# Projections of a hybrid S5 and attention layer: TensorE in program order, late transpositions, gate blocks in between, and a recurrence that steps through PSUM

## The chip, the cores and the metric

The kernel runs on one core of one Trainium2 chip. The metric is the device time of one execution in microseconds (us). Before the change it is 2119.36 us (median of 3 runs, 2116.5 to 2119.44).

## The reference

One layer over 1024 latent tokens and 256 context tokens of width 1024, in fp32. Both are normalised and modulated (shift and scale come from a small "ada" projection of a condition), and one input projection yields everything else:

```
z = modulate(x, ...) @ w_in            # q 1024 | k 1024 | v 1024 | u 512 | gates g 2048
q = rope_2d(rms_norm(q)); k = rope_2d(rms_norm(k))      # 8 heads x 2 maps x 64
y_attn = diff_attention(q, [kc, k], [vc, v])            # two softmax maps per head, subtracted
s_t = a_bar * s_(t-1) + B u_t          # S5: complex diagonal state, 32 groups x 64, both directions
y_s5 = glu(gelu(Re(C s) + D u)) @ w_branch_s5
x = x + ga1 * ((sigmoid(g_s) * y_s5 + sigmoid(g_a) * y_attn) @ w_out)
x = x + ga2 * conv_ffn(modulate(x, ...))                # up, depthwise conv of 3, silu gate, down
```

The context tokens give keys, values and the S5 start state only; they have no q and no gates.

## The kernel before

Every fp32 product is made of three fp32r matmuls: each operand is split in a high and a low part (hi*hi, hi*lo, lo*hi). A weight block of 512 KB is read into `wraw`, ScalarE (ACT) rounds it to `whi` (L596), GpSimd (POOL) subtracts to get `wlo` (L597, 128x1024). The normalised input lies transposed in SBUF as `hTh`/`hTl` (latent) and `cTh`/`cTl` (context).

The part that changes is the first 40% of the program, `phase_a`. It works through column slabs of 512:

- U (10 token tiles of 128), then K in two slabs (20 tiles), V in two slabs (20), Q in two slabs of latent tokens only (16). One tile is one `project` call: 24 matmuls 128x512 into a PSUM bank `z` (L418 to L420).
- A K or Q tile then goes through `qk_post` (L635 to L681). ACT squares it (L640), VectorE (DVE) sums per head (L642), makes 1/sqrt with a Newton step (L643 to L650, ACT's Sqrt at L646 in between), multiplies by the rope tables (L654, L658), POOL adds (L659), ACT and POOL scale (L664, L665), TensorE (PE) transposes four pieces (L669), ACT and DVE split the result (L672, L673), and it goes to memory.
- Beside U and K run the S5 parameters, one quad of groups at a time (`s5_params`): complex products on DVE or POOL (L753 to L758), transposes L846, small matmuls L864. Beside V run the S5 inputs per chunk of 8 tokens (`s5_states_in`, L893, L898, L919).
- The recurrence over 160 chunks is `s5_scan`: 158 steps one after the other, each four DVE operations of 128x64 (L936 to L939), two products with the constants `A8a` and `A8b` and two sums. All operands lie in SBUF. Its calls stand between the V and the Q tiles. `ada_part` (L297, groups of 4 matmuls) stands between the Q tiles.
- The gates: 32 blocks of 24 matmuls (L555 to L557), each followed by a Tanh on ACT (L559). Between them stand the S5 outputs (`s5_out_quad`, L957 to L966, which need the finished scan), and then `s5_tail`: a GELU, the GLU (4x2 GEMMs of 12 matmuls, L1267 to L1269) and the S5 branch projection in "units" of 12 matmuls, each multiplied with a gate read back from memory (L1312).

After it come attention and the feed-forward part, which the change does not touch. The order on each engine is made by a scheduler that simulates the program; `high_priority` lets a piece go first. Attention and feed-forward have PE in the order in which they are written. PSUM has 8 banks: in `phase_a` two for transposes (`ta`, `tb`), five `z`, one `ada`.

Of the kernel before, what the change touches and what calls it, by code (L numbers as in the profile page):

```python
# [10 lines left out]
F32R = mybir.dt.float32r  # L11
# [45 lines left out]
def pack(x, c, ctx, c_ctx, ada_w, ada_b, norm1_w, w_in, b_gate, q_norm_w, k_norm_w,  # L57
# [18 lines left out]
    def perm64(a):  # L76
# [6 lines left out]
             wq[:, :512], wq[:, 512:]] + [w[:, 3584 + 512 * j:4096 + 512 * j] for j in range(4)]  # L83
# [28 lines left out]

    put("wglu", wtiles(np.asarray(glu_w)[0]))
# [25 lines left out]
class Kern:  # L139
# [81 lines left out]
    def consts(self):  # L221
        nc, cp = self.nc, self.cp
        self.small = self.t(cp, [P, NSM], "small")
        self.ident = self.t(cp, [P, P], "ident")
        self.ones = self.t(cp, [P, P], "ones")
# [8 lines left out]
        self.scan_at = 0  # L234
# [52 lines left out]
    def ada_part(self, pool, ps, crep, grp):  # L287
# [3 lines left out]
        for k in range(KT):  # L291
            for h in range(2):
                a = self.t(pool, [P, 2, 512], "araw", 2)
                nc.sync.dma_start(a, self.I["ada"][grp - 1, k][:, 2 * h:2 * h + 2])
                for z in range(2):
                    r0 = 32 * (2 * h + z)
                    nc.tensor.matmul(pa[r0:r0 + 32], crep[:, k], a[:, z], start=k == 0, stop=k == KT - 1,  # L297
                                     tile_position=(0, r0))
                yield
# [13 lines left out]
    def phase_a(self):  # L313
        nc, cp, I = self.nc, self.cp, self.I
        self.psT, self.psT_st = self.pool("psT", space=PSUM)
        ps, ps_st = self.pool("psA", space=PSUM)
        ca, ca_st = self.pool("ca")
# [3 lines left out]
        self.A8a = self.t(ca, [P, 2, G], "A8a")  # L321
        self.A8b = self.t(ca, [P, 2, G], "A8b")
# [88 lines left out]
        def project(tt, W, pz=None, ks=range(KT)):  # L411
            pz = self.t(ps, [P, 512], "z", 5) if pz is None else pz
# [85 lines left out]
        for tt in range(NKT):  # L498
            u = stage(first[tt] if tt < TA else project(tt, W))
            if tt < NT:  # L500
                nc.scalar.dma_start(self.Ud[:, tt], u)
            else:
                nc.scalar.dma_start(self.Ucd[(tt - NT) * P:(tt - NT + 1) * P], u)
            if tt % 2:
                next(params, None)
        zp, zp_st = self.pool("pk")
        self.rope_tables(zp, "K")
        for s in (0, 1):
            W = self.load_slab(wp, s)
# [4 lines left out]
        zp_st.close()  # L514
        for _ in params:
            pass
        xp, xp_st = self.pool("s5x")
        states = self.s5_states_in(xp, ps)
        next(states)
        for s in (2, 3):  # L520
            W = self.load_slab(wp, s)
            for tt in range(NKT):
                v = stage(project(tt, W))
                nc.scalar.dma_start(self.Vd[tt][:, (s - 2) * 512:(s - 1) * 512], v)
                if s > 2 or tt > 3:
                    next(states, None)
                if self.scan_at:
                    self.s5_scan(xp, self.scan_at + 10)
        hc_st.close()
        ap_, ap_st = self.pool("pada", "right")  # L530
        zp, zp_st = self.pool("pq")
        self.rope_tables(zp, "Q")
        adas = (st for grp in (1, 2) for st in self.ada_part(ap_, ps, crep, grp))
        for s in (5, 6):
            W = self.load_slab(wp, s)
            for tt in range(NT):
                self.qk_post(zp, ps, project(tt, W), "Q", s - 5, tt)
                next(adas, None)
                self.s5_scan(xp, self.scan_at + 6)
# [5 lines left out]
        for s in range(7, 11):  # L545
            W = self.load_slab(wp, s)
            for mm in range(4):
                m = (s - 7) * 4 + mm
                for hf in range(2):
                    tok = slice(hf * 512, hf * 512 + 512)  # L550
                    pz = self.t(ps, [P, 512], "z", 5)
                    for k in range(KT):
                        wh = W[0][k // 2][:, k % 2, mm * P:mm * P + P]
                        wl = W[1][k // 2][:, k % 2, mm * P:mm * P + P]
                        nc.tensor.matmul(pz, wh, hTh[k][:, tok], start=k == 0, stop=False)  # L555
                        nc.tensor.matmul(pz, wh, hTl[k][:, tok], start=False, stop=False)
                        nc.tensor.matmul(pz, wl, hTh[k][:, tok], start=False, stop=k == KT - 1)  # L557
                    g = self.t(gp, [P, 512], "stage", 2)
                    nc.scalar.activation(g, pz, AF.Tanh, scale=0.5, bias=self.hbg[:, m:m + 1])  # L559
                    nc.scalar.dma_start(self.Gd[m][:, tok], g)  # L560
                    next(adas, None)
                    if hf and nq < QUADS:
                        if nq % 2 == 0:
                            Yq = self.t(yp, [P, NT, P], "Yq", 1)
                        with self.tc.high_priority():
                            self.s5_out_quad(yp, ps, nq, Yq, xp)
                            nq += 1
# [17 lines left out]
        for _ in tail:  # L585
            pass
# [1122 lines left out]
```

## Time and profile before

| | before |
|---|---|
| median of 3 runs | 2119.36 us |
| profiled execution, device time | 2117.7 us |
| its span, first to last instruction | 2115.9 us |
| PE busy | 2016.6 us (95%) |
| DVE busy | 1364.6 us (64%) |
| POOL busy | 915.0 us (43%) |
| ACT busy | 840.7 us (40%) |
| mean granted TensorE clock | 0.978 |

The span is shorter than the device time by 1.8 us. "Busy" adds up the time in which an engine has an instruction in work. A PE that is busy can still be slow: a matmul at half the clock counts as busy for twice as long. So the stages are read in three numbers: length, PE busy, granted clock.

In the trace the stages lie so: U to about 107 us, K to 283, V to 418, Q to 537, gates to 807 with the S5 outputs at 613 to 673, GLU and units 694 to 821, and then attention.

### The profile page before, as it was taken

Reading aid. Unit: us, or ns where it says so; the run is one execution under the profiler, and the core shown is the slowest. Engines: PE = TensorE matmul, PEld = TensorE weight load, DVE = VectorE, ACT = ScalarE, POOL = GpSimd, SP = SyncE. Lnnn points to the kernel's source line nnn. Section 1 sums busy time; section 2 is a strip of 40 time slices with the busy share of each in tenths; the row PEclk is TensorE's granted clock in tenths of the full one; section 3 lists DMA queues with packets and bytes.
Section 4 is the critical chain, followed back from the end, with each engine's and each line's share of the span. In section 5 each row is a group of like instructions: output and inputs, shape, how many; then the busy total and the mean of one; then the engine's idle time right before and its main releaser. Section 6 shows DMA issues by size and latency. Waiting matters only on the chain.

```text
span 2115.9 us, 29038 instructions
## 1 busy us (share of the span) xinstructions
PE 2016.6 (95%) x10392; PEld 1643.8 (78%) x10392; DVE 1364.6 (64%) x2591; ACT 840.7 (40%) x1509; POOL 915.0 (43%) x1009
## 2 busy tenths in 40 slices
PE   6988999998999999999999989987999999999999
PEld 4766778866678887999999878765888888878887
DVE  6988944799972133888888654468777777752222
ACT  4434424221222312788888611343444443432100
POOL 1466411233311531366666745643544444455321
PEclk9998999999999999999999999987999999999999
DMA  9345575345667326322331135432222222254212
GB/s 325 111 112 140 123 204 182 111 133 163 186 198 232 112 100 225 112 83 78 94 107 53 39 131 177 151 90 70 100 80 79 82 82 79 80 193 129 67 55 93
DMA packets 164624, 262.48 MB, mean 124 GB/s; under 512 B 28672, under 2 KB 92544, under 8 KB 164480
## 3 DMA queue, kind: packets, MB, share of 16 engines
q1 hardware_dynamic: 154400, 242.28, 37.0%
q10 hardware_dynamic: 10080, 18.35, 2.3%
q8 instruction: 82, 1.34, 0.3%
q14 instruction: 62, 0.51, 0.1%
HBM read 188.68 MB, written 71.89 MB: 123 GB/s over the span
## 4 chain that ended last, share of the span: by engine, by line
PE 70%; DVE 21%; DMA 4%; issue 3%; POOL 1%; ACT 1%; SPq 0%; DVEq 0%; ACTq 0%; POOLq 0%
PE ta L1040 7%; PE d L1268 4%; PE d L1269 4%; PE d L1267 4%; PE up L1488 4%; PE up L1489 4%; PE up L1487 4%; PE sc L1240 3%; PE sc L1241 3%; PE z L1487 3%; PE z L1489 3%; PE z L1488 3%; PE tb L1022 3%; DVE X L939 2%; DVE sc L936 2%
## 5 line engine op out<-in xcount | busy, mean ns | idle before, releaser
L1242 DVE TENSOR_REDUCE mx<-sc 128x1 f32<-128x1280 f32 x128 | 190.7, 1491 | 53.3 <-PE sc L1241 52.3
L597 POOL TENSOR_TENSOR wlo<-wraw,whi 128x1024 fp32r<-128x1024 f32 x40 | 97.3, 2449 | 245.8 <-ACT whi L596 243.8
L418 PE MATMUL z<-whi,hTh 128*128 128x512 f32 x448 | 183.1, 413 | 3.6 <-ACT hTh L407 3.6
L419 PE MATMUL z<-wlo,hTh 128*128 128x512 f32 x448 | 181.7, 407 | 0.3 <-POOL wlo L597 0.3
L420 PE MATMUL z<-whi,hTl 128*128 128x512 f32 x448 | 179.9, 403 | 0.0
L995 ACT ACTIVATE e<-sc,mx 128x1280 f32<-128x1280 f32 x128 | 171.9, 1343 | 12.3 <-DVE mx L1242 10.6
L1664 DVE SCALAR_TENSOR_TENSOR x1b<-d,modT,x1b 128x512 f32<-128x512 f32 x80 | 59.8, 750 | 181.3 <-PE d L1269 181.3
L1040 PE MATMUL ta<-V,at 128*128 128x128 f32 x1280 | 168.1, 275 | 0.7 <-ACT at L1029 0.7
L1040 PEld LDWEIGHTS ta<-V,at 128*128 128x128 f32 x1280 | 155.4, 191 | 1.0 <-ACT at L1029 0.9
L1240 PE MATMUL sc<-K,q 128*128 128x512 f32 (+1 forms) x384 | 147.7, 385 | 0.8 <-ACT e L995 0.8
L1480 POOL TENSOR_TENSOR pl<-s,ph 128x512 fp32r<-128x512 f32 x44 | 65.0, 1479 | 182.5 <-ACT ph L1479 182.5
L1268 PE MATMUL d<-g,whi 128*128 128x512 f32 x352 | 139.8, 397 | 3.1 <-DVE g L1636 3.1
L1685 DVE SCALAR_TENSOR_TENSOR y<-up,small,y 128x896 f32<-128x896 f32 (+1 forms) x176 | 123.7, 744 | 29.5 <-ACT y L1680 28.1
L1267 PE MATMUL d<-g,whi 128*128 128x512 f32 x352 | 139.5, 396 | 0.0
L1269 PE MATMUL d<-g,wlo 128*128 128x512 f32 x352 | 139.3, 396 | 0.0
L1241 PE MATMUL sc<-K,q 128*128 128x512 f32 (+1 forms) x384 | 131.9, 358 | 0.0
L1255 POOL TENSOR_TENSOR wlo<-wraw,whi 128x1024 fp32r<-128x1024 f32 (+1 forms) x36 | 74.9, 2087 | 122.5 <-ACT whi L1254 111.6
L418 PEld LDWEIGHTS z<-whi,hTh 128*128 128x128 f32 x448 | 87.1, 194 | 33.1 <-issue 9.8
L1660 POOL TENSOR_TENSOR wlo<-wraw,whi 128x640 fp32r<-128x640 f32 (+2 forms) x40 | 56.3, 1407 | 116.3 <-ACT whi L1659 115.3
L555 PE MATMUL z<-hTh,whi 128*128 128x512 f32 x256 | 102.4, 400 | 0.0
L420 PEld LDWEIGHTS z<-whi,hTl 128*128 128x128 f32 x448 | 87.3, 195 | 19.3 <-issue 1.0
L419 PEld LDWEIGHTS z<-wlo,hTh 128*128 128x128 f32 x448 | 87.5, 195 | 17.4 <-POOL wlo L597 0.7
(490 smaller groups left out, 5509.0 us busy)
## 6 DMA issues: line engine op xcount, KB each, us to landing
wraw<-in_wup_dram SPq DMA_DIRECT2D x46, 512.0 KB
wraw<-in_win_dram SPq DMA_DIRECT2D x44, 512.0 KB
araw<-in_ada_dram SPq DMA_DIRECT2D x32, 512.0 KB
q<-Qd SPq DMA_DIRECT2D x128, 128.0 KB
Kd<-st SPq DMA_DIRECT2D x80, 128.0 KB
K<-Kd SPq DMA_DIRECT2D x16, 640.0 KB
Fd<-y SPq DMA_DIRECT2D x20, 512.0 KB
graw<-Fd SPq DMA_DIRECT2D x20, 512.0 KB
```

The costliest lines, as they stand in the source:

```text
L418: nc.tensor.matmul(pz, hh, wh, start=k == 0, stop=False)
L419: nc.tensor.matmul(pz, hh, wl, start=False, stop=False)
L420: nc.tensor.matmul(pz, hl, wh, start=False, stop=k == KT - 1)
L995: nc.scalar.activation(em, S[i]["sc"][m][:, :LK], AF.Exp, bias=S[i]["mx"][:, m:m + 1], accum_out=S[i]["l1"] if m else S[i]["l0"])
L1040: nc.tensor.matmul(PO[p][:, j * P:j * P + P], AT[p, kt // 2][:, kt % 2, j * P:j * P + P], W[:, kt], start=kt == 0, stop=kt == NKT - 1)
L1240: nc.tensor.matmul(sc[:, a:b], Q[0][:, m, qs], K[m][:, a:b], start=True, stop=False)
L1241: nc.tensor.matmul(sc[:, a:b], Q[1][:, m, qs], K[m][:, a:b], start=False, stop=True)
L1242: nc.vector.tensor_reduce(S["mx"][:, m:m + 1], sc[:, :LK], axis=AX.X, op=OP.max, negate=True)
L1267: mm(o, W[0][:, k], ah[k], start=k == 0, stop=False)
L1268: mm(o, W[0][:, k], al[k], start=False, stop=False)
L1269: mm(o, W[1][:, k], ah[k], start=False, stop=k == n - 1)
L1487: mm(o, W[0][:, k], bh[k], start=k == 0, stop=False)
```

## The change

1. From U to the end of Q, PE runs in the order in which the program is written (`manual_schedule`), instead of an order that the scheduler finds.
2. The four transposes of a K or Q tile (`qk_turn`) are written two tiles later (`LAG = 2`, the list `later`).
3. The gates become a generator with a weight layout of its own (`wg`: 16 blocks of 512 KB, one weight split for two gate blocks). Eight gate blocks are written between K tiles, four between Q tiles, one behind Q; 19 of 32 stay for the end.
4. `s5_params` is cut in a part for the vector engines (`vec`) and one for PE (`mul`), with two buffers in between.
5. After three V tiles the PSUM pool is opened anew with four `z` banks and one scratch bank `scr`. In it lie the recurrence's constants (`A8p`, 128x128), its products (`scT`) and small vectors of the Q tiles (`qkp`). A step of the recurrence becomes three DVE operations: one product of 128 elements (state in SBUF, constants and result in PSUM), two sums of 64 elements (SBUF and PSUM to SBUF).
6. The Newton step is written with one product fewer between two SBUF operands; `qk_post` of Q stands under `high_priority`; `t1` has three buffers, `t2` one.

The core of the diff:

```diff
-        for tt in range(NKT):
-            u = stage(first[tt] if tt < TA else project(tt, W))
+        LAG = 2
+        later = []
+        def unit(part=None):
+            if part is not None:
+                later.append(part)
+            if len(later) > LAG or (part is None and later):
+                later.pop(0)()
+        gates = self.gates(wp, lambda: self.t(ps, [P, 512], "z", nz), hTh, hTl)
+        with self.tc.manual_schedule(engines={ET.PE}):
...
             for s in (0, 1):
                 W = self.load_slab(wp, s)
                 for tt in range(NKT):
-                self.qk_post(zp, ps, project(tt, W), "K", s, tt)
-                if tt % 4 == 3:
+                    unit(self.qk_post(zp, ps, project(tt, W), "K", s, tt))
+                    if tt in (1, 3, 5, 6):
+                        next(gates)
                     next(params, None)
...
+            scr = self.t(ps, [P, 512], "scr", 1)
+            self.A8p = scr[:, 0:128].rearrange("p (j i g) -> p j i g", j=2, i=2)
+            self.scT = [scr[:, 128 * j:128 * j + 128].rearrange("p (j i g) -> p j i g", j=2, i=2) for j in (1, 2)]
+            self.qkp = [[scr[:, 384 + 32 * b + 8 * j:392 + 32 * b + 8 * j] for j in range(2)] for b in range(4)]
+            nc.vector.tensor_copy(self.A8p, self.A8)
...
             for s in (5, 6):
                 W = self.load_slab(wp, s)
                 for tt in range(NT):
-                self.qk_post(zp, ps, project(tt, W), "Q", s - 5, tt)
+                    pz = project(tt, W)
+                    with self.tc.high_priority():
+                        turn = self.qk_post(zp, ps, pz, "Q", s - 5, tt)
+                    unit(turn)
+                    if tt in (2, 4):
+                        next(gates)
+                        next(adas, None)
+                        self.s5_scan(xp, self.scan_at + 6)
                     next(adas, None)
                     self.s5_scan(xp, self.scan_at + 6)
+            next(gates)
...
-            E(t1, X[:, i - 1], self.A8a, op=OP.mult)
-            E(t2, X[:, i - 1, ::-1], self.A8b, op=OP.mult)
-            E(X[:, i], X[:, i], t1, op=OP.add)
-            E(X[:, i], X[:, i], t2, op=OP.add)
+            t = self.scT[i % 2]
+            E(t, X[:, i - 1, None].to_broadcast([P, 2, 2, G]), self.A8p, op=OP.mult)
+            E(X[:, i], X[:, i], t[:, 0], op=OP.add)
+            E(X[:, i], X[:, i], t[:, 1, ::-1], op=OP.add)
```

On PE, in the K stage, the order before has the transposes of a tile (L669, out of `t_321`) between the matmuls of a later projection tile (`z_1877`), and the small matmuls of the S5 parameters (L864) within it too:

```order
407 L420 MATMUL z_1877<-whi_1470,hTl_25_114 128x512
408 L418 MATMUL z_1877<-whi_1470,hTh_18_107 128x512
409 L669 MATMUL tb_1659<-ident_74,t_321_1647 128x128
410 L419 MATMUL z_1877<-wlo_1471,hTh_18_107 128x512
411 L669 MATMUL tb_1659<-ident_74,t_321_1647 128x128
412 L420 MATMUL z_1877<-whi_1470,hTl_26_115 128x512
413 L669 MATMUL tb_1659<-ident_74,t_321_1647 128x128 x2
414 L864 MATMUL ada_946<-ca_908,blk_939 32x128 x16
415 L864 MATMUL ada_946<-sc_895,dup_941 32x16 x8
```

Now a projection tile stands whole, and behind its last matmul (row 366) come the four transposes of the tile two places before it (L724) and then a whole quad of the parameters (L912, L921):

```order
366 L426 MATMUL z_1284<-whi_1110,hTl_29_118 128x512
367 L724 MATMUL tb_1334<-ident_74,t_235_1152 128x128 x4
368 L912 MATMUL ada_1347<-ident_74,ba_1067 128x128 x4
369 L912 MATMUL z_1355<-ident_74,ba_1067 128x128 x4
370 L921 MATMUL z_1363<-ca_1068,blk_1083 32x128 x16
371 L921 MATMUL z_1363<-sc_1055,dup_1085 32x16 x8
372 L424 MATMUL z_1392<-whi_1092,hTh_14_103 128x512
```

On DVE, where the first Q tile comes (`z_866` before), its reduction stands behind some 41 of the 158 steps, and its operations lie between those of the next steps:

```order
767 L936 TENSOR_TENSOR sc1_788_4173<-X_549_2989,A8a_13_96 128x64
768 L937 TENSOR_TENSOR sc2_789_4174<-X_549_2989,A8b_14_97 128x64
769 L642 TENSOR_REDUCE qv_868_4474<-sq_867_4472 128x8
770 L654 TENSOR_TENSOR t1_871_4484<-z_866_4447,CQ_852_4417 128x512
771 L938 TENSOR_TENSOR X_549_2989<-X_549_2989,sc1_788_4173 128x64
772 L658 TENSOR_TENSOR t2_872_4486<-z_866_4447,SQ_853_4418 128x512
```

Now the two rope products of the first Q tile (`t1_779`, `t2_780`) stand at rows 733 and 734, and its reduction at row 846, behind 80 steps of three operations (L1001 to L1003):

```order
843 L1001 TENSOR_TENSOR scr_614_3360<-X_615_3368,scr_614_3360 128x128
844 L1002 TENSOR_TENSOR X_615_3368<-X_615_3368,scr_614_3360 128x64
845 L1003 TENSOR_TENSOR X_615_3368<-X_615_3368,scr_614_3360 128x64
846 L693 TENSOR_REDUCE scr_614_3360<-sq_775_4559 128x8
847 L694 TENSOR_SCALAR qv_776_4561<-scr_614_3360 128x8
848 L705 TENSOR_TENSOR t1_789_4637<-z_784_4600,CQ_760_4505 128x512
```

PE has ten projection tiles and one group of ada matmuls between the last S5 input (row 1354) and the transposes of that first Q tile (row 1597); before the first S5 output (row 2171) 17.3 gate blocks stand on PE, where it were 10. On ACT, the Tanh of a gate and the Sqrt of a K or Q tile belong to different function tables; the order has 30 table loads in the program now, and had 6. One gate of the K stage on ACT (L635 is its Tanh, L697 the Sqrt of a tile):

```order
95 L697 ACT_TABLE_LOAD
96 L697 ACTIVATE qt_264_1316<-qv_261_1311 128x8
...
103 L715 ACTIVATE t1_282_1430<-t1_282_1430,qr_280_1423 128x64 x6
104 L627 CAST whi_327_1692<-wraw_326_1690 128x1024
105 L635 ACT_TABLE_LOAD
106 L635 ACTIVATE stage_288_1480<-z_287_1455,hbg_7_81 128x512
```

The Tanh takes its place in ACT's row between the pieces of `qk_post`, with one load in front of it and one in front of the next Sqrt.

## Rows read from the trace of the kernel before

**Rows 1.** The page's first part: busy us, share of the span, instructions.

```profile
PE 2016.6 (95%) x10392; PEld 1643.8 (78%) x10392; DVE 1364.6 (64%) x2591; ACT 840.7 (40%) x1509; POOL 915.0 (43%) x1009
```

**Rows 2.** Stages: from:to, busy us (instructions) by engine, clock, DMA share, GB/s.

```profile
107.00:283.00 176.00, 153.41 (x963) 118.38 (x962) 158.12 (x316) 72.38 (x211) 105.23 (x104) 0.93 0.52 136
283.00:387.00 104.00, 103.21 (x579) 86.96 (x578) 37.74 (x78) 39.29 (x101) 9.80 (x4) 1.00 0.55 163
418.00:537.00 119.00, 109.43 (x470) 74.12 (x470) 116.54 (x389) 23.11 (x49) 45.67 (x37) 0.97 0.53 157
537.00:613.00 76.00, 71.08 (x297) 48.67 (x294) 72.15 (x266) 17.60 (x24) 23.01 (x12) 0.96 0.63 198
748.00:821.00 73.00, 73.00 (x321) 60.06 (x320) 15.54 (x17) 9.40 (x15) 17.05 (x13) 1.00 0.45 147
```

**Rows 3.** PE's waits, 107 to 283 us: us in total, times, longest.

```profile
PE ta L669 <- ACT t L664: 10.6, 7, 4.4
PE ada L864 <- ACT wi L848: 4.2, 1, 4.2
```

**Rows 4.** PE's waits, 418 to 613 us.

```profile
PE ta L669 <- POOL t L665: 5.6, 3, 4.2
PE ada L297 <- DMA araw<-in_ada_dram: 4.0, 2, 3.2
```

**Rows 5.** PE alone around one of them: start, us, instruction, [idle before <-releaser].

```profile
191.25 0.47 PE L669 MATMUL ta<-ident,t 128*128 128x128 f32 x1 [4.39 <-ACT t L664]
...
196.43 0.63 PE L418 MATMUL z<-whi,hTh 128*128 128x512 f32 x1
196.85 0.60 PE L419 MATMUL z<-wlo,hTh 128*128 128x512 f32 x1
```

**Rows 6.** The seven stretches at half clock (first, last, sum): from:to, PE busy, clock.

```profile
159.80:166.60 6.80, 5.54 (x14) 0.50 0.06 21
...
555.70:562.50 6.80, 5.53 (x17) 0.50 0.69 189
sum 37.40, PE 33.20; mean PE 4.74
```

**Rows 7.** DVE by line, 107 to 283 us: busy, mean ns | idle before.

```profile
L642 DVE TENSOR_REDUCE qv<-sq 128x8 f32<-128x512 f32 x20 | 13.5, 674 | 3.5 <-ACT sq L640 3.5
```

**Rows 8.** DVE in order of time: the start of two steps of the recurrence.

```profile
385.08 0.23 DVE L936 TENSOR_TENSOR sc<-X,A8a 128x64 f32<-128x64 f32 x1
...
385.87 0.23 DVE L936 TENSOR_TENSOR sc<-X,A8a 128x64 f32<-128x64 f32 x1
```

**Rows 9.** DVE by line, 418 to 620 us.

```profile
L936 DVE TENSOR_TENSOR sc<-X,A8a 128x64 f32<-128x64 f32 x125 | 43.1, 345 | 3.2
```

**Rows 10.** DVE by line, 407 to 424 us.

```profile
L936 DVE TENSOR_TENSOR sc<-X,A8a 128x64 f32<-128x64 f32 x8 | 4.9, 613 | 0.3
```

**Rows 11.** POOL by line, 407 to 424 us.

```profile
L597 POOL TENSOR_TENSOR wlo<-wraw,whi 128x1024 fp32r<-128x1024 f32 x4 | 9.5, 2411 | 58.3 <-ACT whi L596 58.3
```

**Rows 12.** DVE by line, 566 to 600 us: sums in SBUF, PSUM operand `tb`, none in PSUM.

```profile
L938 DVE TENSOR_TENSOR X<-X,sc 128x64 f32<-128x64 f32 x38 | 10.5, 275 | 0.0
L310 DVE TENSOR_TENSOR modT<-tb,small 128x16 f32<-128x16 f32 x2 | 0.2, 164 | 0.0
L1373 DVE TENSOR_SCALAR hga<-modT 128x8 f32<-128x8 f32 x1 | 0.2, 161 | 0.0
```

**Rows 13.** DVE by line, 20 to 107 us: one operation of 128 elements.

```profile
L385 DVE TENSOR_SCALAR sq<-ident,n1h 128x128 fp32r<-128x128 f32 x5 | 1.1, 278 | 0.0
```

**Rows 14.** ACT by line, 107 to 283 us.

```profile
L672 ACT CAST st<-ta 128x512 fp32r<-128x512 f32 x10 | 5.8, 584 | 0.0
L646 ACT ACT_TABLE_LOAD x1 | 1.3, 1283 | 0.0
```

**Rows 15.** DVE in order of time, start of attention.

```profile
832.43 0.69 DVE L1312 SCALAR_TENSOR_TENSOR gate<-gate,tb 128x512 f32<-128x512 f32 x1 [5.34 <-DMA gate<-Gd]
```

**Rows 16.** POOL, splitting the GLU's result, in order of time.

```profile
743.91 4.55 POOL L1260 TENSOR_TENSOR h5l<-gth,h5h 128x512 fp32r<-128x512 f32 x3 [0.36 <-DVE h5h L1259]
```

More of the change, by code (lines that the diff above doesn't have):

```diff
@@ L82, in pack @@
     slabs = [wk[:, :512], wk[:, 512:], w[:, 2048:2560], w[:, 2560:3072], w[:, 3072:3584],
-             wq[:, :512], wq[:, 512:]] + [w[:, 3584 + 512 * j:4096 + 512 * j] for j in range(4)]
+             wq[:, :512], wq[:, 512:]]
     put("win", np.stack([s.reshape(2, 4, P, 512).transpose(0, 2, 1, 3) for s in slabs]))
@@ L544, in phase_a @@
         tail = None
[L545 to L567, printed above, removed]
-                            if nq % 2 == 0:
-                                self.s5_transpose(yp, ps, Yq, nq // 2 - 1)
-                        if nq == QUADS:
-                            for _ in adas:
-                                pass
-                            ap_st.close()
-                            yp_st.close()
-                            xp_st.close()
-                            tail = self.s5_tail(ps)
-                    elif tail:
-                        next(tail, None)
@@ new lines, in phase_a @@
+        for _ in gates:
+            next(adas, None)
+            if nq < QUADS:
+                next(adas, None)
+                if nq % 2 == 0:
+                    Yq = self.t(yp, [P, NT, P], "Yq", 1)
+                with self.tc.high_priority():
+                    self.s5_out_quad(yp, ps, nq, Yq, xp)
+                    nq += 1
+                    if nq % 2 == 0:
+                        self.s5_transpose(yp, ps, Yq, nq // 2 - 1)
+                if nq == QUADS:
+                    for _ in adas:
+                        pass
+                    ap_st.close()
+                    yp_st.close()
+                    xp_st.close()
+                    tail = self.s5_tail(ps)
+            else:
+                next(tail, None)
@@ L586, in phase_a, with gates @@
             pass
+    def gates(self, wp, bank, hTh, hTl):
+        nc = self.nc
+        for m in range(16):
+            blk = lambda x: x.rearrange("p a b -> p (a b)").rearrange("p (k n) -> p k n", k=KT)
+            raw = self.t(wp, [P, 2, 512], "wraw", 3)
+            nc.sync.dma_start(blk(raw), self.I["wg"][m])
+            h = self.t(wp, [P, 2, 512], "whi", 5, F32R)
+            l = self.t(wp, [P, 2, 512], "wlo", 5, F32R)
+            nc.scalar.copy(h, raw)
+            nc.gpsimd.tensor_tensor(l, raw, r32(h), op=OP.subtract)
+            W = blk(h), blk(l)
+            for hf in range(2):
+                tok = slice(hf * 512, hf * 512 + 512)
+                pz = bank()
+                self.gemm(pz, W, [x[:, tok] for x in hTh], [x[:, tok] for x in hTl])
+                g = self.t(self.gp, [P, 512], "stage", 2)
+                nc.scalar.activation(g, pz, AF.Tanh, scale=0.5, bias=self.hbg[:, m:m + 1])
+                nc.scalar.dma_start(self.Gd[m][:, tok], g)
+                yield
     def load_slab(self, wp, s, qs=(0, 1, 2, 3)):
@@ L872, in s5_params @@
             nc.sync.dma_start(self.Td[q], kq)
+        prev = None
+        for q in range(QUADS + 1):
+            yield
+            cur = vec(q) if q < QUADS else None
+            yield
+            if prev:
+                mul(q - 1, *prev)
+            prev = cur
         sp_st.close()
```

166 lines of the change are left out of this document (94 added, 72 removed).

## The prediction

> **What bounds the kernel now.** I read the page's first part, then the table of stages, then PE's waits in the stages that lose time, then DVE's rows by line. TensorE is busy for 2016.6 of 2115.9 us [rows 1], so the end is set by PE's work, its idle time, and its clock. The table of stages says where it loses: 22.6 us idle between 107 and 283 us (K), 0.8 us between 283 and 387 (V), 9.6 us between 418 and 537 and 4.9 us between 537 and 613 (Q and the end of the recurrence), nothing in the gates [rows 2]. In the K and Q stages DVE is the busier engine: 158.1 us of 176 and 116.5 of 119 [rows 2]. PE's waits name the same chain: transposes that wait for ACT or POOL to scale a tile, which wait for DVE's small operations, and a few transfers [rows 3, 4]. Each longer wait has a second price. Behind an idle 4.39 us a matmul starts 0.42 us after the one before it [rows 5]; at full clock it is 73.0 us over 320, 0.228 us [rows 2] in the stretch of gates and units. [...]
>
> So there are 22.6 + 10.6 = 33.2 us to be had in K, 14.5 + 6.0 = 20.5 us in Q, and nothing in V. More than 54 us can come only from less work, and PE's work hardly changes.
>
> **The change part by part.** All sums are against the profiled execution, 2117.7 us, its span and 1.8 us around it; it lies 1.7 us under the median, within what the runs differ by.
>
> *Gates in the K stage, transpositions two tiles late, parameters in two halves.* PE's work at full clock in K is 153.4 - 10.6 = 142.8 us. Eight gate blocks of 24 x 0.228 = 5.47 us add 43.8 and make 186.6 us; they are missing later, so they cost nothing in sum. DVE keeps its 158 us, and four more weight splits on POOL of 2.41 us each [rows 11] may hold it up by up to 10. DVE goes from the busier engine to 85 or 90% of PE. A tile's transposes come two tiles of 5.47 us and often a gate later, 11 to 16 us, against a chain of about 4 us when nothing is in its way (the reduction alone is 0.674 us [rows 7], two rope products as long, then seven small operations). What remains is lumps: a quad of the S5 parameters on DVE is some 20 operations of 512 and 64 elements in one go, and PE can no longer take other work past a transpose that waits, since everything behind it, projections and gates, waits too. The bounds are 0 (all 33.2 us gained) and 33 (the lumps stop PE as before). I take 11 us left, five lumps on DVE of about 2 us each, without a fall of the clock: minus 22.
>
> *Function tables.* Gates among K and Q tiles bring 24 more table loads of 1.283 us [rows 14], 31 us on ACT, which is busy 72 of 176 us in K [rows 2]. Each makes a tile's chain longer by 1.3 us, in a cover of 11; I take 0, and 31 us as the bound if none were hidden.
>
> *V in program order.* Each of 8 quads has transposes, their copy on ACT, and small matmuls, in place. A copy of 512 elements takes 0.584 us [rows 14], and two in a row per quad would show 8 x 2 x 0.584 = 9 us at most; the projection tile between them hides part. I take 4, from 0 to 9. The new PSUM pool with four z banks, which waits until the old one is empty, is within that.
>
> *The recurrence.* Before, an undisturbed step starts every 0.79 us [rows 8]. Beside weight splits of 2.41 us on POOL [rows 11], operations with two SBUF operands take 0.613 us in the mean [rows 10] and not 0.23, and over the Q stage 0.345 [rows 9]. The reduction and the rope products, with an operand in PSUM or only one, do not stretch: 0.674 us in the mean [rows 7]. The new step has three operations with one SBUF operand each. No row shows a product written to PSUM and read from it by DVE. An operation of 128 elements takes 0.278 us [rows 13], sums of 64 some 0.25 us each start to start (0.275 with the overlap [rows 12]): I estimate 0.28 + 0.034 + 0.25 + 0.25, about 0.82 us (0.034 is the space between a short operation and one that needs its result, from the step of 0.79). Bounds: 0.65 (as if the large product cost like a small one) and 1.2 (three operations of 0.4, as those that are disturbed now).
>
> Whether it pays is decided by one place. In the new order the first Q tile's reduction stands behind 80 steps on DVE. PE has ten tiles and one ada group before that tile's transposes: 10 x 5.47 + 1 = 55.7 us. DVE has 80 x 0.82 = 65.6 us, two rope products (1.4), the rest of the tile's chain (4) and a start about 1.5 us late: 72.5. PE stands for some 17 us, and the clock costs another 3. Behind it PE has 13 tiles, 9.3 gate blocks, 16 groups of transposes and the ada matmuls, about 142 us, and DVE 78 x 0.82 + 16 x 3.4 = 118 us: PE sets the pace. So Q loses 20 in place of 20.5 us: 0. At 0.65 us a step it loses 4 + 0, a gain of 16; at 1.2 it loses 48 + 3, and costs 30.
>
> [...]
>
> *The end.* Of 22 gate blocks that lay beside the S5 outputs, the GLU and the units, 14.7 remain for the outputs and the tail, and some five cover the GLU and the units. The splits of the GLU's result take POOL 4.55 us for three [rows 16], 6 us for a half of the tokens, and stand in front of the units. I take 5 us that show, from 0 to 12. The wait for a gate from memory (5.34 us on DVE [rows 15]) is still hidden by the first scores or comes to the same.
>
> Sum: -22 + 0 + 4 + 0 + 5 = -13, so 2117.7 - 13 = 2104.7; with the median for the scale about 2105 us.
>
> **The rivals.**
> - *More is recovered.* The step takes 0.65 to 0.7 us, or K's lumps vanish in the cover: 33 + 4 in place of -22 + 4 for K and V gives about 2094; with Q's 16 us too 2078. For it: K's DVE has 28 us of room. Against it: the 80 steps are a fixed block.
> - *The recurrence through PSUM is slow, and PE stands behind it.* Place: the first Q tile's transposes, with all of PE's later work queued behind. At 1.2 us a step it costs 30 in Q: 2117.7 - 13 + 30 = 2135. It decides from the step at which Q's loss grows by 13 us, (13 / 80) + 0.82, 0.98 us. For it: no row shows DVE's way through PSUM and back. [...] Against it: an operand in PSUM costs 0.003 us [rows 12]. [...]
> - *Table loads on the chain.* ACT is in order too; a Tanh whose gate is not ready holds a tile's scaling back. All 24 loads showing: -13 + 31, 2136. Against it: ACT's 41%, and two tiles of cover.
> - *PE's order doesn't matter.* The K stage is bound by DVE before and after (158 of 176 us): the lumps cost 33 us in any order, -13 + 22 = 2127, or, with 16 us from a faster step, 2111 and no more than a small gain.
>
> **How the numbers follow.** The forecast has 0.46 (its own range 2094 to 2115), more recovered 0.24, the slow recurrence 0.15, table loads 0.03, PE's order 0.12. A measurement of this kernel can tell 0.2%, 4.2 us, from no change. Faster holds nearly all of the first two and a third of the last, 0.71; same a little of each, 0.11; slower 0.18. The range of 8 in 10 goes from the middle of the larger gain (2078) to the place between no change and the slow step, 2130.
>
> **What would show it.** Right: in the K stage PE busy at 96% or more with 1.00 granted, while DVE falls under 95%; steps that start every 0.8 us also while POOL splits weights; one wait of PE of 10 to 20 us at the first transposes of Q, with half clock behind it; the first S5 output some 20 us later than 613 us, with 7.3 more gate blocks done (40 us of work less the 18 gained until then). Wrong: steps of 1 us or more; waits of PE at transposes all through K; or no wait at the first Q tile, which would make the gain twice as large.

## The result: 22 us slower, and the profile after

The changed kernel takes 2141.6 us (median of 4 runs, 2137.0 to 2143.1), the kernel before on the same chip 2119.4; the ratio is 1.010, 95% interval 1.0077 to 1.0122. The forecast was 2105 us, with a range of 2078 to 2130. The profiled execution took 2137.0 us, its span 2135.2 (2115.9 before); so the traces account for 19.3 us, the medians differ by 22.2.

The page's first part of the changed kernel, to lay beside [rows 1]:

```profile
PE 2001.3 (94%) x10392; PEld 1645.4 (77%) x10392; DVE 1310.6 (61%) x2434; ACT 872.9 (41%) x1533; POOL 904.4 (42%) x1009
```

Its stages as in [rows 2], but cut at its own borders: K, V, Q with the rest of the recurrence, the end up to attention, and last the worst stretch of Q.

```profile
101.10:310.80 209.70, 191.19 (x1192) 155.54 (x1191) 155.42 (x308) 99.41 (x224) 112.18 (x108) 0.93 0.48 143
310.80:450.80 140.00, 136.63 (x683) 114.19 (x682) 68.95 (x191) 50.06 (x126) 22.87 (x14) 1.00 0.43 132
450.80:669.80 219.00, 171.84 (x775) 125.76 (x774) 144.50 (x501) 52.75 (x81) 71.62 (x47) 0.91 0.50 156
669.80:859.90 190.10, 186.71 (x932) 151.97 (x930) 59.47 (x72) 47.09 (x69) 54.94 (x37) 0.99 0.58 190
472.60:499.90 27.30, 5.12 (x14) 4.21 (x15) 23.28 (x89) 1.28 (x3) 2.27 (x2) 0.50 0.07 20
```

PE stands idle for 47 us of the 219 in Q, where it stood for 14.5 us in [rows 2], and runs at half clock (0.50 granted) in the stretch of the last row. The borders in both traces are the first matmul of K, V and Q, the first S5 output with states (L966 before) and the first transposes of attention. Since gates moved between stages, each stage is shown without its own gate blocks (their count x 5.47 us):

| stage, us without its gate blocks | before | changed | forecast | measured |
|---|---|---|---|---|
| up to K | 98.6 | 101.1 | not in the sum | +2.5 |
| K | 163.0 | 209.7 - 43.8 = 165.9 | -22 | +2.9 |
| V | 148.9 | 140.0 | +4 | -8.9 |
| Q to the first S5 output | 202.9 - 55.2 = 147.7 | 219.0 - 50.9 = 168.1 | 0 | +20.4 |
| end | 227.0 - 119.8 = 107.2 | 190.1 - 80.4 = 109.7 | +5 | +2.5 |
| attention and after | 1275.5 | 1275.3 | 0 | -0.2 |

The last column adds up to 19.2 of the span's 19.3 us. Two terms failed and made the kernel slower, Q and K; V came out shorter, where 4 us more were forecast.

What Q lost is more than its 20.4 us. Its idle time grew by 32.7 us (47.2 for 14.5), while PE's busy time in it without gates fell by 12.3 (171.8 - 50.9 for 188.4 - 55.2). The largest piece that the rows name is the ada matmuls of Q and the end, 11 us less for the same 128:

```profile
L297 PE MATMUL ada<-araw,crep 128*32 128x512 f32 x128 | 33.5, 619 | 4.0 <-DMA araw<-in_ada_dram 4.0
L302 PE MATMUL ada<-araw,crep 128*32 128x512 f32 x128 | 22.4, 662 | 0.0
```

The first line is from before, the second from the changed kernel (both 0 to 860 us). The list of the change leaves out that `ada_part` now writes the matmuls of two transfers behind one another: a row of eight takes 1.07 us on PE, a row of four took 1.05.

PE's waits from 413 to 670 us, for [rows 4], and the first of them on PE in order of time:

```profile
PE tb L724 <- POOL t L716: 31.3, 5, 26.0
PE ta L724 <- POOL t L716: 13.0, 3, 7.7
PE ta L309 <- ACT stage L306: 2.8, 1, 2.8
```

```profile
494.78 1.11 PE L724 MATMUL tb<-ident,t 128*128 128x128 f32 x4 [26.00 <-POOL t L716]
```

DVE in order of time: one step of the recurrence to the next, the first rope product of Q, and the end of the 80 steps.

```profile
429.89 0.30 DVE L1001 TENSOR_TENSOR scr<-X,scr 128x128 f32<-128x128 f32 x1
430.22 0.22 DVE L1002 TENSOR_TENSOR X<-X,scr 128x64 f32<-128x64 f32 x1
430.48 0.22 DVE L1003 TENSOR_TENSOR X<-X,scr 128x64 f32<-128x64 f32 x1
430.73 0.29 DVE L1001 TENSOR_TENSOR scr<-X,scr 128x128 f32<-128x128 f32 x1
...
457.42 0.69 DVE L705 TENSOR_TENSOR t<-z,CQ 128x512 f32<-128x512 f32 x1 [6.57 <-ACT sq L689]
...
489.40 0.22 DVE L1003 TENSOR_TENSOR X<-X,scr 128x64 f32<-128x64 f32 x1
489.66 0.69 DVE L693 TENSOR_REDUCE scr<-sq 128x8 f32<-128x512 f32 x1
490.38 0.17 DVE L694 TENSOR_SCALAR qv<-scr 128x8 f32<-128x8 f32 x1
```

The step starts every 0.84 us (0.82 estimated), beside POOL's weight splits too (no operation of it takes over 0.30). It is 80 of them, from 414.8 us, that PE stands behind: the reduction starts at 489.7, the transposes at 494.8, and PE was there at 468.8. The 80 steps alone take 67.1 of these 74.9 us. Behind 43 of them DVE's order has the two rope products of the first Q tile, and there the recurrence stands still for 6.6 us, until ACT has squared that tile (456.7 to 457.3 us), which itself stood for the tile's projection on PE. The lines of DVE from 413 to 610 us, for [rows 9]:

```profile
L1001 DVE TENSOR_TENSOR scr<-X,scr 128x128 f32<-128x128 f32 x158 | 46.6, 295 | 5.2
L1003 DVE TENSOR_TENSOR X<-X,scr 128x64 f32<-128x64 f32 x158 | 34.9, 221 | 5.4
L1002 DVE TENSOR_TENSOR X<-X,scr 128x64 f32<-128x64 f32 x158 | 34.8, 220 | 5.3
L705 DVE TENSOR_TENSOR t<-z,CQ 128x512 f32<-128x512 f32 x12 | 8.3, 691 | 12.6 <-ACT sq L689 8.7 <-ACT qt L697 3.9
```

The recurrence takes DVE 116.3 us (158 x 0.736), and it took 198.5 (158 x 1.256, its four lines in the trace before). The part that was made faster is faster, and the kernel is slower. In K, for [rows 3], PE's waits from 100 to 320 us are others than before, and nearly as long (18.9 us in all for 21.2 from 107 to 283):

```profile
PE z L425 <- POOL wlo L648: 6.6, 4, 3.2
PE z L921 <- DVE ca L895: 4.3, 1, 4.3
PE tb L724 <- ACT t L715: 3.9, 1, 3.9
PE ta L724 <- ACT t L715: 3.2, 1, 3.2
```

### The profile page after: what moved, and what is told of

The parts are those of the page before. It is cut to its first block, busy times and chain, and to the rows that moved or that the text cites. A ratio compares the mean times of both kernels' runs of the same rounds, so it can differ in the third digit from the quotient of the medians.

```text
span 2135.2 us, 28879 instructions
## 1 busy us (share of the span) xinstructions
PE 2001.3 (94%) x10392; PEld 1645.4 (77%) x10392; DVE 1310.6 (61%) x2434; ACT 872.9 (41%) x1533; POOL 904.4 (42%) x1009
## 4 chain that ended last, share of the span: by engine, by line
PE 65%; DVE 3%; issue 2%; DMA 1%; ACT 0%; POOL 0%; SPq 0%; DVEq 0%; ACTq 0%; POOLq 0%
PE ta L1104 7%; PE d L1332 4%; PE d L1333 4%; PE d L1331 4%; PE up L1552 4%; PE up L1553 4%; PE up L1551 4%; PE sc L1304 4%; PE sc L1305 3%; PE z L1553 3%; PE z L1551 3%; PE z L1552 3%; PE z L1331 3%; PE z L1332 3%; PE z L1333 3%; PE tb L1086 3%
## 5 line engine op out<-in xcount | busy, mean ns | idle before, releaser
L424 PE MATMUL z<-whi,hTh 128*128 128x512 f32 x448 | 183.1, 409 | 4.3 <-ACT hTh L413 3.6
L1104 PE MATMUL ta<-V,at 128*128 128x128 f32 x1280 | 168.1, 275 | 0.7 <-ACT at L1093 0.7
L648 POOL TENSOR_TENSOR wlo<-wraw,whi 128x1024 fp32r<-128x1024 f32 x24 | 57.7, 2420 | 147.4 <-ACT whi L647 116.1
```

What stands on the lines that cost most here:

```text
L424: nc.tensor.matmul(pz, hh, wh, start=k == 0, stop=False)
L1104: nc.tensor.matmul(PO[p][:, j * P:j * P + P], AT[p, kt // 2][:, kt % 2, j * P:j * P + P], W[:, kt], start=kt == 0, stop=kt == NKT - 1)
```

## The experiments

All times are medians; the kernel before, run beside them, took 2119.2 to 2121.3 us. "Front" is the number of steps of the recurrence that stand on DVE in front of the first Q reduction, "between" those from one Q reduction to the next, "behind" those after the last one; a fraction is a step of which some operations stand there. The interval in the last column is that of the ratio.

| run | front, between, behind | Q without gates | us | ratio to before (95%) |
|---|---|---|---|---|
| before | 41.5, 0.25 to 9, 56.25 | 147.7 | 2119 | |
| changed | 80, 6 to 12, 0 | 168.1 | 2141.6 | 1.0077 to 1.0122 |
| 5 and 4 steps written | 40, 4 to 8, 42 | 139 | 2128.8 | 1.0030 to 1.0055 |
| 7 and 5 steps written | 56, 5 to 10, 7 | 154 | 2130.5 | 1.0030 to 1.0060 |
| step in SBUF, 4 operations | 46.75, 3.5 to 12.5, 20.25 | 144 | 2117.8 | 0.9971 to 0.9993 |
| step in SBUF, 3 operations | 43, 3 to 12, 27 | 143 | 2112.8 | 0.9958 to 0.9981 |
| vectors of Q in SBUF | 43, 3 to 12, 28 | 121 | 2087.0 | 0.9830 to 0.9861 |
| the same, DVE in written order | 80, 6 to 12, 0 | 162 | 2142.5 | 1.0079 to 1.0136 |
| all three edits | 43, 3 to 10, 30 | 116 | 2075.3 | 0.9778 to 0.9804 |

**Fewer steps in front (written 5 and 4).**

```diff
-                        self.s5_scan(xp, self.scan_at + 10)
+                        self.s5_scan(xp, self.scan_at + 5)
...
-                    self.s5_scan(xp, self.scan_at + 6)
+                    self.s5_scan(xp, self.scan_at + 4)
```

> The changed kernel with two constants changed: 5 steps of the recurrence per V tile in place of 10, 4 per call between the Q tiles in place of 6. On DVE the first Q tile's reduction then stands behind 40 steps (80 before), later ones behind 4 to 8 (6 to 12), and 42 steps follow the last Q tile. Theory A (the order: DVE has too many steps in front of and between the Q tiles, and PE, in program order, stands behind them): the wait of 26 us at the first Q transposes goes, the waits at later ones fall from 19 us to under 6; 2141.6 falls by 18 to 28 us, to 2114 to 2124. Theory B (steps through PSUM, PE's order as such, or table loads cost it): the time stays above 2134.

Measured 2128.8 us, neither theory's time. Q does what theory A said: no wait at the first Q tile, 29 us less. But the end takes 125 us without gates, in place of 110: 31.1 of the 32 gate blocks now stand before the first GLU matmul, and less than one is left to cover the GLU. The longest of PE's waits from 662 to 850 us in that run:

```profile
PE tb L1331 <- DVE h5h L1323: 7.6, 2, 4.0
```

**Written 7 and 5.** The constants alone again.

> The changed kernel with 7 steps of the recurrence per V tile and 5 per call between the Q tiles (10 and 6 in the change, 5 and 4 in the first run): 56 steps in front of the first Q reduction, 5 or 10 between later ones, 7 behind the last. On PE 28.5 gate blocks stand before the first GLU matmul (26.8 in the change, 31.1 in the first run). Theory (steps in front of the Q tiles cost waits of PE at their transposes, steps behind them cost gate blocks, which then are missing beside the GLU): 56 steps of 0.84 us fit under ten tiles, no wait over 3 us at the first Q tile; the end from the first S5 output to attention costs 110 to 118 us without its gates, not 125; the whole 2116 to 2126. If the first run's wait at the end came from its late recurrence alone and not from the gates used up, this is 2110 to 2116.

Measured 2130.5 us, over the expected range. The end keeps to it (114 us), the first wait does not (5.8 us), and waits at later tiles stay (29.7 us at L724 in all). The expected sum left out that the recurrence stands still at the first Q tile's rope product, 6.6 us here too. In both runs the order follows the written constants to the step (8 x 5, 8 x 7), which a scheduler that is free to choose has no reason to do.

**The step in SBUF.** Four operations as before; then three, with 5 and 4 written (the diff shows the edit to the step of three).

```diff
-            t = self.scT[i % 2]
-            E(t, X[:, i - 1, None].to_broadcast([P, 2, 2, G]), self.A8p, op=OP.mult)
+            t = self.t(xp, [P, 2, 2, G], "sct", 2)
+            E(t, X[:, i - 1, None].to_broadcast([P, 2, 2, G]), self.A8, op=OP.mult)
```

> The changed kernel with the recurrence's step as it was: four operations of 64 elements with all operands in SBUF. The order then has 46 steps in front of the first Q reduction, 4 to 12 between later ones. Theory A: a step takes 0.79 us alone and over 1.0 us in the mean (POOL stretches it); 46 steps take 45 to 58 us, about what PE needs for its ten tiles, so the wait of 26 us goes, waits at later tiles stay; 2141.6 falls by 8 to 20 us. Theory B, its part on PSUM (the step through PSUM is slower than the old one): steps under 0.84 us in the mean, and a fall of over 20 us. If the step through PSUM is worth something by itself, this is slower than the run with fewer steps in front.

> The changed kernel with 5 and 4 steps as in the first run, and the step of three operations with its constants and products in SBUF in place of PSUM: 43 steps in front of the first Q reduction, 3 to 12 between, 27 behind the last. If operands in PSUM keep POOL's weight splits from stretching the step, single operations here take up to 2.4 us while POOL splits weights, and the step is 0.84 us when POOL is idle and about 1.0 in the mean; if PSUM made no difference, all steps take 0.84 us. Time: 2114 to 2128 in both cases, since these 158 x 0.2 us lie partly in DVE's idle time.

Measured 2117.8 and 2112.8 us. The first is 24 us faster than the changed kernel, more than theory A's 20, but its steps take 1.24 us busy in the mean, so that theory B's part on PSUM does not hold. The second lies just under its range. DVE's lines of the second, from 410 to 650 us:

```profile
L1001 DVE TENSOR_TENSOR sct<-X,A 128x128 f32<-128x128 f32 x158 | 70.9, 448 | 4.3
L1003 DVE TENSOR_TENSOR X<-X,sct 128x64 f32<-128x64 f32 x158 | 56.4, 357 | 4.3
L1002 DVE TENSOR_TENSOR X<-X,sct 128x64 f32<-128x64 f32 x158 | 46.8, 296 | 4.2
```

The same three operations take 1.10 us busy in place of 0.736, single ones up to 2.49 us. A slower step, and a kernel faster by 16 us than the run with the same constants and the step in PSUM. And here the order is not tied to the constants (46.75 with 80 written, 43 with 40). What differs is that the recurrence no longer touches the tile `scr`, in which the Q tiles' vectors lie.

**The vectors of Q out of the shared tile.**

```diff
-        vp, rp = self.qkp[self.qkn % 4] if kind == "Q" else (v, self.t(zp, [P, 8], "qi", 2))
+        vp, rp = v, self.t(zp, [P, 8], "qi", 2)
```

> The changed kernel with one edit: the small vectors of the Q tiles (sum, 1/sqrt) lie in SBUF as those of the K tiles do, not in the scratch bank of the recurrence; steps of 10 and 6 as in the change, the step through PSUM as it is. The order on DVE then has 43 steps in front of the first Q reduction, 3 to 12 between, 28 behind the last, and 80 or 40 or 56 no longer follow the constants. Theory (sharing one PSUM tile between the recurrence and the reductions ties both to the order in which they are written, and that puts the 80 steps in front): the wait of 26 us goes, a step stays at 0.74 us busy and 0.84 start to start, and the whole is 18 to 28 us faster than the change, 2114 to 2124. Rival (the step through PSUM costs by itself, since the two runs with the step in SBUF were the fast ones): 2128 or more.

Measured 2087.0 us, 55 us faster than the changed kernel and far beyond the expected range; the rival falls. Its rows on DVE (410 to 640 us) and all of PE's waits (413 to 670 us):

```profile
L1001 DVE TENSOR_TENSOR scr<-X,scr 128x128 f32<-128x128 f32 x158 | 46.6, 295 | 4.2
L694 DVE TENSOR_SCALAR qv<-qv 128x8 f32<-128x8 f32 x16 | 12.3, 771 | 0.0
```

```profile
PE ta L309 <- ACT stage L306: 3.1, 1, 3.1
PE ada L302 <- DMA araw<-in_ada_dram: 1.0, 1, 1.0
PE z L425 <- POOL wlo L648: 0.7, 1, 0.7
```

No transposition of a Q tile is waited for. I had expected back only what Q had lost. Without gates it takes 121 us, 47 less than in the changed kernel and 27 less than before; of these 27, 10 are idle time (4.8 for 14.5 us) and 17 a shorter busy time on PE (169.5 - 53.8 for 188.4 - 55.2, half clock included), so that not all of it is owed to the step. The vectors in SBUF are stretched by POOL (0.771 us for L694, in PSUM 0.17), and no wait of PE comes of it.

**Order or place?** The same kernel, DVE held to the written order from the S5 inputs to the end of Q (the block is put under `manual_schedule(engines={ET.PE, ET.DVE})`).

> The run with the Q tiles' small vectors in SBUF (2087 us), with DVE held to the order in which the program is written from the S5 inputs to the end of Q: 80 steps in front of the first Q reduction and 6 or 12 between later ones, as in the change, but no vector shares the scratch bank. Theory (the order alone is the cost, the shared bank only its cause): the wait of 20 us or more at the first Q transposes is back, and the whole is 2130 to 2146. Rival (vectors in PSUM are slow by themselves): 2085 to 2100.

Measured 2142.5 us, with no vector in PSUM. PE's waits from 455 to 675 us:

```profile
PE tb L727 <- POOL t L719: 17.9, 3, 15.2
PE ta L727 <- DVE scr L1004: 16.0, 3, 10.8
```

The written order alone costs what the change had lost, 55 us against the same kernel with a free order, and the shared tile is what had imposed it. It does not lose them in quite the same places: the first Q tile is waited for 15.2 us, less than the expected 20, since its rope products now stand behind its reduction and the recurrence doesn't stop for them; Q takes 162 us in place of 168, and the end 118 in place of 110. That the two times agree to 1 us is in part chance. And the edit holds all of DVE's operations in these stages, not only the steps. The counter-test for the vectors' place is the kernel of 2101.2 us that is described under "All edits together", with the step in SBUF, where the order is free in any case:

> The run of 2101 us (step in SBUF, parameters two tiles later, ada transposes later) with the Q tiles' small vectors in SBUF too, so that nothing of Q lies in the scratch bank; the order on DVE stays the same (43 in front, 3 to 10 between, 30 behind). It shows what the place of the vectors is worth without the order: theory, within 6 us of 2101, slower rather than faster, since POOL can stretch operations on vectors in SBUF (0.8 us in place of 0.17 for the longest line). Rival (vectors in PSUM cost): 2090 or less.

Measured 2098.0 us (2096.8 to 2099.4) against 2101.2 (2098.0 to 2102.2): the vectors' place is worth some 3 us at most, and PSUM does not come out as the better one.

**K.** First without the eight gates, then with the parameters' small matmuls later.

```diff
-                    if tt in (1, 3, 5, 6):
-                        next(gates)
```

> The changed kernel without the eight gate blocks between the K tiles; they come with the others at the end. Theory A (in program order the gates bring as many waits as they cover: ACT's rounding of a gate's weights waits for their DMA with a K tile's scaling behind it, and the splits of the next slab come late): the K stage takes 158 to 168 us, 0 to 8 less than the 166 it takes now without the gates' own 43.8; the whole stays within 2134 to 2144. Rival (the gates cover DVE's lumps, as I predicted): the K stage takes 175 us or more, and the whole 2150 or more.

Measured 2162.8 us, and K takes 183.1 us: the rival, which was my forecast, holds. The gates cover 17 us (183.1 against 165.9); without them K, with PE in program order, is 20 us longer than the 163.0 of the kernel before. PE's waits in K of that run:

```profile
PE z L425 <- POOL wlo L646: 7.2, 3, 3.5
PE tb L722 <- POOL bb L806: 6.5, 1, 6.5
PE z L919 <- POOL ca L808: 5.6, 1, 5.6
PE z L919 <- DVE ca L893: 4.8, 1, 4.8
```

```diff
-                    next(params, None)
+                    if s or tt not in (2, 3):
+                        next(params, None)
```

> The changed kernel with the small matmuls of the S5 parameters two tiles later in K, nothing else. Theory (in program order they hold PE behind DVE and POOL): K takes 194 to 197 us in place of 210, and the whole is 12 to 18 us faster than the change, 2123 to 2130. Rival (K's gain is lost again at the 80 steps): 2134 or more.

> The run with 7 and 5 steps, and in the K stage the small matmuls of the S5 parameters two tiles later (two calls left out at the third and fourth tile). Theory (in program order PE stands for a quad's products that POOL and DVE have not finished: 5 to 6 us idle at 129 to 134 us and 6.8 us of half clock behind it): that wait goes, K is 6 to 9 us shorter, and the whole as much against the run without this edit. Rival (DVE and POOL are the bound there, and the wait moves to the next quad): within 3 us.

Measured 2127.8 us (14 less than the changed kernel, as expected), and 2117.7 with 7 and 5 steps (13 less than without the edit, more than I expected). K with its gates takes 194.2 and 194.8 us, in place of 209.7. In the first run only these waits are left in K; those at L921 and at the transposes are gone:

```profile
PE z L425 <- POOL wlo L649: 7.3, 3, 2.7
PE z L424 <- ACT whi L648: 1.2, 1, 1.2
```

**Function tables and program order.** `AF.Identity` for the gates' `AF.Tanh`; then `if True:` for `with self.tc.manual_schedule(engines={ET.PE}):`.

> The changed kernel with Identity in place of the gates' Tanh, so that ACT loads 5 tables in place of 30; the gates' values are other ones. Theory A: table loads lie in the cover of two tiles, 0 to 4 us. Theory B, its part on tables: 24 loads of 1.283 us on the chain from a tile to its transposes, 10 to 30 us faster.

> The changed kernel with PE ordered by the scheduler through U, K, V and Q as before the change, all else as in the change (gates in between, transposes written two tiles late, recurrence through PSUM with its 10 and 6 steps). Theory (program order on PE costs some 20 us in K, which the eight gates there give back, and the 80 steps hold the first Q tile in any order): K takes 150 to 160 us without its gates' 43.8, against 166; the wait at the first Q transposes stays over 15 us, since the order is fixed when the kernel is built, with gates of the end possibly put in front of it; the whole 2122 to 2136. Rival (program order itself costs nothing): within 4 us of 2141.6.

Measured 2136.8 us without the tables (2134.5 to 2140.5, against 2137.0 to 2143.1): theory B is out, and whether 24 table loads cost anything is not shown, since the times overlap, and K and Q without gates take 166.8 and 166.9 us in that trace (165.9 and 168.1 in the changed kernel's). Measured 2121.2 us with PE's order from the scheduler, 20 less and just under the expected range: K takes 203.3 - 43.8 = 159.5 us, and Q 167, for it has other waits than for transposes. PE was given ada matmuls ahead of them that wait for their transfer, and projections that wait for a free bank `z` (455 to 664 us):

```profile
PE z L424 <- DVE t L709: 17.0, 2, 9.4
PE ada L302 <- DMA araw<-in_ada_dram: 10.4, 6, 4.0
```

Its profiled execution (2126.5 us) was the longest of its ten, and the traces place only 10.5 of the 20 us, most of them in K (6.5) and V (3.2).

**All edits together.** Vectors in SBUF, parameters two tiles later, and a `yield` between the copy of an ada group and its transposes. The second run has the step in SBUF in place of the vectors, and 5 and 4 written.

> Three edits to the changed kernel: the Q tiles' small vectors in SBUF, the parameters' matmuls two tiles later in K, and the transposes of an ada group one call later than the copy that they need (PE stood up to 8 us for that copy). If the terms add: 26 to 40 us faster than the change, 2100 to 2114. Faster than both kernels if so.

> The run with the step of three operations in SBUF, and with the parameters' matmuls two tiles later and the ada transposes one call later. Against the run with both edits and the step in PSUM (the orders on DVE are nearly the same, 43 steps in front in both) it shows what PSUM operands are worth: 158 steps take about 0.25 us longer here, and if DVE is what PE waits for in Q this is 5 to 15 us slower than that run; if not, within 4 us. The whole 2096 to 2112.

Measured 2075.3 us (2073.9 to 2076.7), faster than both kernels, 0.979 of before, and 25 us under the expected range; and 2101.2. With nearly the same order on DVE, the step's operands in PSUM are worth 26 us, or 23 against the 2098.0 of the run that has the vectors in SBUF too: more than I had expected, and all of it in Q (116 us without gates, against 141 and 142). PE's longest waits of the first from 101 to 612 us, through K, V and Q:

```profile
PE z L426 <- POOL wlo L650: 13.7, 8, 4.0
PE tb L987 <- ACT ut L962: 2.3, 1, 2.3
PE ada L302 <- DMA araw<-in_ada_dram: 0.8, 1, 0.8
```

**The lag and program order, on that kernel.** `LAG = 0`; then the scheduler's order on PE.

> The run with all three edits (2075 us) with the transposes of a tile written right behind its own projection (no lag), PE in program order. Theory (the lag is what makes program order bearable: each of 36 tiles would stand for a chain of about 4 to 5 us, gates only in part in between): 36 x 4 us and half clock behind many, 120 to 230 us slower, 2195 to 2305. If the gates and other tiles covered it, under 2110.

> The run with all three edits (2075 us) with PE ordered by the scheduler again in place of program order. In the change itself that was 20 us faster. Theory (program order was a loss there because matmuls were written too early; once they are written where their operands are ready it costs nothing): within 8 us of 2075. Rival (the scheduler's order is better by itself): 2065 or less; rival (program order with a lag is better by itself): 2085 or more.

Measured 2375.6 us, worse than expected: without a lag PE stands 30 times for the chain behind a tile, 187 us in all from 100 to 800 us.

```profile
PE ta L726 <- ACT t L717: 67.8, 9, 12.0
PE tb L726 <- ACT t L717: 46.4, 9, 7.9
PE tb L726 <- POOL t L718: 41.7, 7, 6.5
PE ta L726 <- POOL t L718: 30.9, 5, 8.2
```

And 2082.7 us: program order is 7 us better than the scheduler's here (expected: within 8), while it was 20 us worse in the changed kernel.

## Why the prediction was wrong

- **What bounds the kernel: right, but "PE's work hardly changes" was not.** PE's idle time, 133.9 us for 99.3 over the span, grew by more than the kernel lost, nearly all of it in Q. Its busy time fell by 15.3 us, the ada matmuls alone by 11, and this hides part of the loss. Attention and after it came out alike, as forecast. The 10.6 us in K and 6.0 in Q that the forecast adds for the clock are half of PE's busy time in the stretches of [rows 6] (21.2 and 12.0 us). The traces show somewhat less: at 0.50 granted a matmul of 128x512 starts every 0.43 us, at 1.00 every 0.23 (before at 195.6 us and at 761, changed at 497 and at 501), so that a matmul takes 1.9 times as long and not twice, and by that ratio 9.9 and 5.6 us were lost.
- **The recurrence: the step was right, the wait behind it was not.** "PE stands for some 17 us" was 26.0. The sum set 72.5 us of DVE against 55.7 of PE. Counted in the trace from PE's first matmul behind the S5 inputs (412.5 us), PE needs 56.3 us to the transposes and DVE 82.3: a start 2.3 us late, 67.1 for the 80 steps, 1.2 for the rope products, 5.1 for the rest of the tile's chain, and 6.6 in which it stands still at the rope products for the tile. That last term the sum put at nothing; the order showed it, with the rope products in the middle of the 80 steps.
- **"Behind it PE [...] sets the pace" failed.** I compared sums, 142 us of PE against 118 of DVE, as if all of PE's work could lie beside DVE's. DVE took from 489.7 to 608.7 us, 119 us where the sum has 118, but with 6 or 12 steps in front of each tile's reduction, and 5.5 of PE's 9.3 gate blocks, 30 us, came only behind the recurrence's end. So PE waited 18 us more at later Q transposes and 3 at those of an ada group. Measured +20.4 for 0.
- **The rival with the right place had the wrong price.** "PE stands behind it" at the first Q transposes was named, but as a matter of steps slower than 0.98 us. Steps took 0.84. The number of steps in front decides, and the order that I printed showed it: 80, exactly 8 x 10. I read it as given and did not ask why it had been 41 with the same constants. The answer is the shared tile, shown by the run with the vectors in SBUF (2087) and by that with the written order (2142.5).
- **K: that gates cover waits was right, what remains was not.** "I take 11 us left": PE's waits are nearly as long as before, and K is 2.9 us longer where 22 less were forecast. The gates do cover 17 us, but without them the changed K is 20 us longer than before, and I had counted before's 33 us of waits as what remains to be won, without asking what the scheduler's interleaving had already hidden. The parameters' matmuls, which I named, were most of it: two tiles later, K is 15 us shorter. Program order itself costs K 6.5 us against the scheduler's, gates included; with the parameters two tiles later it is 5 us better there (194.3 against 199.3).
- **V** came out at -8.9 for +4. Part of this is the border: before, the matmuls of the last parameter quads (L864 until 298 us) and the 4.2 us wait of [rows 3] (at 275 us) lay behind V's first matmul, and now they are in K. Taken together K and V were forecast at -18 and measured at -6.0. The rest was not tried alone.
- **Function tables and the end** came out as taken: no cost of the tables that is clear of noise for 0, and 2.5 us for 5.
- **The signs.** Steps of 0.84 us and a wait at the first Q transposes came as said. In K PE was busy for 91% at a clock of 0.93, not 96% and 1.00, and the first S5 output came 56 us later than 613, not 20.
- **Contention: right for the step, not for every operation with one SBUF operand.** With one SBUF operand no operation of the step exceeds 0.30 us (changed kernel), with two it reaches 2.49 (the step of three in SBUF). But L694, a `tensor_scalar` with one SBUF operand, takes 0.771 us in the mean with the vectors in SBUF. The way through PSUM, which no row of before had shown, does not make the step slow: it starts every 0.84 us, and an operation of 64 elements takes 0.220 us with a PSUM operand and 0.23 without [rows 8]. In the run with 5 and 4 written and all operands in SBUF, the same step starts every 0.84 us too where its operations are not stretched:

```profile
420.44 0.29 DVE L1001 TENSOR_TENSOR sct<-X,A 128x128 f32<-128x128 f32 x1
421.28 0.29 DVE L1001 TENSOR_TENSOR sct<-X,A 128x128 f32<-128x128 f32 x1
```

## What to carry to other kernels

When small results share a tile with a long chain, a scheduler that tracks tiles may order one after the other: count in the order how many links stand in front of each, look for the written constants in that count, and look for an operation among the links that waits for another engine, since the whole chain stands with it. A faster operation is worth nothing until the order lets its time be used: here the step through PSUM was worth some 23 us once the order was free, and in the changed kernel the order took more than that away. Program order on an engine is as good as the places at which its waiting instructions are written; first find what they wait for, then move those two tiles.

## What had not been expected of the hardware

A chain of dependent DVE operations through PSUM cost no more here than one through SBUF, 0.84 us a step in both: from the start of the product of 128 elements to that of the sum that reads it 0.33 us pass, between the sums of 64 elements 0.26, against 0.25 between the sums in SBUF before. Operations of 8 elements in SBUF are stretched like long ones beside POOL: in the run with the vectors in SBUF L694 takes 0.771 us in the mean (0.17 with its source in PSUM). In K of the changed kernel, where its vector lies in SBUF too, it takes 0.16 us with POOL idle, 0.85 to 1.17 beside POOL's rope sum of 128x512 (L710, 1.26 to 1.30 us), and 2.17 beside a weight split of 2.35 (L628). Ada matmuls of two transfers written behind one another took PE 1.07 us for eight, where four by themselves took 1.05.
